# The last MLP group by seven half-size products too, and the second layer's norm on four engines

## The chip, the cores and the metric

The kernel runs on one core of one Trainium2 chip. The time is device microseconds of one execution, the median of the runs; the profile is of one further execution. The core has five engines with in-order queues of their own: TensorE (PE in the rows; PEld is its weight load), VectorE (DVE), ScalarE (ACT), GpSimd (POOL) and SyncE (SP), which issues the transfers.

## The reference, cut to what matters

The program is a two-layer trunk over 512 tokens of width 1024. Each layer has a mixer and an MLP, with a norm before each and a last norm behind the second layer. The change touches the MLPs, the norm before the second mixer (fox) and the last norm.

```python
def rmsnorm(x, g):
    xf = x.astype(jnp.float32)
    y = xf * lax.rsqrt(jnp.mean(xf * xf, axis=-1, keepdims=True) + RMS_EPS)
    return (y * g.astype(jnp.float32)).astype(x.dtype)

def sqrelu_mlp(h, w1, w2):
    a = jax.nn.relu(h @ w1)
    return (a * a) @ w2

def reference(x, ...):
    h = x
    for layer in range(DEPTH):
        hn = rmsnorm(h, mix_norm[layer])
        ...
        h = h + sqrelu_mlp(rmsnorm(h, mlp_norm[layer]), mlp_w1[layer], mlp_w2[layer])
    return rmsnorm(h, final_norm)
```

w1 is 1024 x 4096, w2 is 4096 x 1024, all in float32.

## The kernel before, in words

Every product is done as three matmuls in a reduced 32-bit format (mm3, L124 to L129): each operand is split into a high half (a copy that rounds, on ACT) and a low half (the operand less its high half, on DVE or POOL), and high x high, high x low and low x high are added up in PSUM. Weights come in by 512 KB loads on SP; split (L89, L92) makes both halves of a plain piece.

The residual stays in SBUF as four tiles x0 to x3 of 128 tokens x 1024. The stages follow each other: mixer of layer 0 (to about 295 us), its MLP (to about 635), the fox mixer of layer 1 (to about 875), its MLP (to about 1218), the tail. The order of instructions on each engine is set by the framework's scheduler from the program, its dependencies and a model of durations; prio() (L781) gives what is issued inside it precedence. An engine works through its queue in that order.

An MLP (mlp, L925) goes through 8 groups of 512 hidden columns. up(s) makes a group's activations in four blocks of 128 columns: 24 matmuls into a PSUM tile "acc", then relu on ACT (L971), a product with the row of inverse norms on POOL (L972), a square on ACT (L974). down(s) multiplies them by 512 rows of w2. For the groups 0 to 6 it does a 2 x 2 block product by seven half-size products in place of eight: combos makes sums and differences of the activations on POOL (L990 to L995) and splits each into halves on ACT (L980) and DVE (L398); weights makes those of w2 with additions on DVE (L1029) and splits on ACT (L1023) and DVE (L1024). A product is two tiles of tokens by 6 matmuls of 512 columns (L1069); where a PSUM bank holds a finished piece of the result, DVE adds it to the residual (L1077). Banks have the tags s, o, pt and acc. The products' order is 2, 1, 6, 7, 4, 5, 3, and product 2 is added up over the groups in two banks "pt". Group 7 is done by down_plain, a plain product, 4 tiles of tokens one behind the other, with additions at L1116. In the second layer finish makes the last norm of a tile behind its additions: inv_rms squares on ACT with a sum (L158), finds the inverse root by Newton steps of one column on DVE (L160 to L167), POOL multiplies by the final gain (L1086) and scales (L1089), and the last tile is scaled by ACT and DVE (L1093, L1094).

The norm before fox (norm_t, L370, and norm, L196) does one square of 1024 on ACT, the Newton steps, and two scalar_tensor_tensor on DVE (L200), which scale by the inverse norm and multiply by the gain at once. Then TensorE transposes (L386) and ACT and DVE make the halves xhi and xlo (L390, L391), from which fox's first projection starts.

## Time and profile before

| | us |
|---|---|
| median of 3 runs | 1227.72 (1227.18 to 1228.32) |
| the profiled execution | 1227.37 |
| its span | 1225.7 |
| TensorE busy in it | 1206.8 (98%) |
| DVE busy | 960.1 (78%) |
| ACT busy | 656.2 (54%) |
| POOL busy | 470.5 (38%) |

The span is the time from the first to the last instruction of the profiled execution; 1.67 us of its time lie outside. The mean granted clock of TensorE in it is 0.998 of full speed. Busy shares are means over stages with different limits.

### The profile page before, as it was taken

What the parts mean: (1) busy time and instruction counts of PE and PEld (TensorE: products, weight loads), DVE (VectorE), ACT (ScalarE), POOL (GpSimd) and SP (SyncE); (2) the same over time, 40 slices, a digit from 0 to 9 for tenths busy, and PEclk for the clock granted to TensorE, in tenths of its full rate; (3) what the DMA queues carried; (4) which work ended last, traced back from release to release, by engine and by line L of the source; (5) the groups of instructions that cost most, each with busy time, mean ns of one, the idle gap of its engine ahead of it and who ended that gap; (6) DMA issues with size and microseconds to landing.
All of it is one profiled execution on the core that took longest, in us unless ns stands there. A gap on an engine that the chain in (4) does not pass through costs nothing.

```text
span 1225.7 us, 17221 instructions
## 1 busy us (share of the span) xinstructions
PE 1206.8 (98%) x6215; PEld 1023.2 (83%) x6215; DVE 960.1 (78%) x1654; ACT 656.2 (54%) x1195; POOL 470.5 (38%) x483
## 2 busy tenths in 40 slices
PE   9999999999999999999999999999999999999997
PEld 7889987887888888888888898988788888888886
DVE  6877678788877987798875678548887798779875
ACT  6457666675554455445425666546455445544542
POOL 3534457542443224322103644435154323432314
PEclk9999999999999999999999999999999999999999
DMA  8962232130633333324015211321363333332201
GB/s 238 338 177 53 87 103 79 52 112 20 170 105 110 92 106 104 110 90 121 27 34 149 72 54 55 87 87 52 107 171 106 111 90 105 105 111 92 88 1 69
DMA packets 141968, 123.78 MB, mean 101 GB/s; under 512 B 6403, under 2 KB 117163, under 8 KB 141884
## 3 DMA queue, kind: packets, MB, share of 16 engines
q1 hardware_dynamic: 141724, 122.45, 34.0%
q8 instruction: 49, 0.80, 0.3%
q14 instruction: 35, 0.29, 0.1%
q10 hardware_dynamic: 160, 0.23, 0.1%
HBM read 120.27 MB, written 7.64 MB: 104 GB/s over the span
## 4 chain that ended last, share of the span: by engine, by line
PE 92%; DVE 5%; issue 1%; ACT 1%; DMA 1%; POOL 0%; DVEq 0%; ACTq 0%
PE acc L127 17%; PE acc L129 17%; PE acc L128 17%; PE s L1069 12%; PE o L1069 6%; PE s L415 4%; PE pt L437 3%; PE pt L1069 3%; PE o L450 2%; PE o L449 2%; DVE whl L92 1%; PE s L127 1%; PE s L128 1%; PE s L129 1%; PE pt L386 1%
## 5 line engine op out<-in xcount | busy, mean ns | idle before, releaser
L129 PE MATMUL acc<-xhi,whl 128*128 128x512 f32 (+1 forms) x768 | 294.9, 384 | 1.3 <-POOL whl L92 0.8
L127 PE MATMUL acc<-xhi,whl 128*128 128x512 f32 (+1 forms) x768 | 293.7, 383 | 0.7 <-DVE Q L400 0.5
L128 PE MATMUL acc<-xlo,whl 128*128 128x512 f32 (+1 forms) x768 | 293.3, 382 | 0.0
L92 DVE TENSOR_TENSOR whl<-raw,whl 128x1024 fp32r<-128x1024 f32 (+2 forms) x113 | 165.5, 1468 | 83.4 <-ACT whl L89 79.3
L972 POOL TENSOR_TENSOR r<-r,yrow 128x512 f32<-128x512 f32 x64 | 97.5, 1524 | 318.4 <-ACT r L971 315.9
L89 ACT ACTIVATE whl<-raw 128x1024 fp32r<-128x1024 f32 (+1 forms) x139 | 144.7, 1048 | 47.8 <-PE acc L129 31.1
L129 PEld LDWEIGHTS acc<-xhi,whl 128*128 128x128 f32 x768 | 144.6, 188 | 29.5 <-POOL whl L92 1.2
L127 PEld LDWEIGHTS acc<-xhi,whl 128*128 128x128 f32 x768 | 144.3, 188 | 28.3 <-PE acc L129 0.9
L1069 PE MATMUL s<-whl,sp 128*128 128x512 f32 x672 | 167.6, 390 | 0.0
L128 PEld LDWEIGHTS acc<-xlo,whl 128*128 128x128 f32 x768 | 144.8, 188 | 26.5
L1069 PEld LDWEIGHTS s<-whl,sp 128*128 128x128 f32 x672 | 126.2, 188 | 26.5
L1023 ACT ACTIVATE whl<-w 128x1024 fp32r<-128x1024 f32 x98 | 103.6, 1060 | 72.0 <-PE s L1069 44.3
L1024 DVE TENSOR_TENSOR whl<-w,whl 128x1024 fp32r<-128x1024 f32 x98 | 134.2, 1371 | 8.6 <-ACT whl L1023 8.6
L420 ACT ACTIVATE P<-P,sst 128x128 f32<-128x128 f32 (+3 forms) x160 | 88.9, 557 | 39.3 <-DVE sst L419 37.4
L971 ACT ACTIVATE r<-acc 128x512 f32<-128x512 f32 x62 | 37.1, 598 | 118.2 <-PE acc L129 118.2
L1069 PE MATMUL o<-whl,sp 128*128 128x512 f32 x336 | 88.8, 391 | 0.0
L439 ACT ACTIVATE PTh<-pt 128x512 fp32r<-128x512 f32 (+1 forms) x120 | 61.4, 523 | 49.4 <-PE pt L437 48.3
L440 DVE TENSOR_TENSOR PTl<-pt,PTh 128x512 fp32r<-128x512 f32 (+1 forms) x120 | 70.4, 596 | 20.7 <-ACT PTh L439 19.9
L92 POOL TENSOR_TENSOR whl<-raw,whl 128x1024 fp32r<-128x1024 f32 x26 | 64.3, 2476 | 54.6 <-ACT whl L89 54.0
L1029 DVE TENSOR_TENSOR w<-w,w 128x1024 f32<-128x1024 f32 x56 | 83.1, 1485 | 1.5 <-DMA w<-in_mlp_w 0.6
L422 POOL TENSOR_SCALAR P<-P,sst 128x128 f32<-128x128 f32 (+1 forms) x96 | 52.3, 550 | 70.7 <-DVE sst L421 64.8
L1077 DVE TENSOR_TENSOR x<-s,x 128x512 f32<-128x512 f32 x112 | 75.0, 682 | 3.0 <-PE s L1069 3.0
(279 smaller groups left out, 2429.3 us busy)
## 6 DMA issues: line engine op xcount, KB each, us to landing
raw<-in_mlp_w SPq DMA_DIRECT2D x72, 512.0 KB
w<-in_mlp_w SPq DMA_DIRECT2D x56, 512.0 KB
raw<-in_odd_w_in SPq DMA_DIRECT2D x22, 512.0 KB
raw<-in_even_w_in SPq DMA_DIRECT2D x20, 512.0 KB
band<-bias_dram SPq DMA_DIRECT2D x24, 256.0 KB
bias_dram<-bias_rows SPq DMA_DIRECT2D x16, 320.0 KB
raw<-in_even_w_out SPq DMA_DIRECT2D x8, 512.0 KB
raw<-in_odd_w_out SPq DMA_DIRECT2D x8, 512.0 KB
```

The costliest lines, as they stand in the source:

```text
L89: nc.scalar.activation(hl[:, 0, :n], raw[:, :n], AF.Copy)
L92: eng.tensor_tensor(hl[:, 1, :n], raw[:, :n], hl[:, 0, :n].bitcast(F32), op=ALU.subtract)
L127: mm(ps, ahl[0], bhl[0], start=first, stop=False)
L128: mm(ps, ahl[0], bhl[1], start=False, stop=False)
L129: mm(ps, ahl[1], bhl[0], start=False, stop=last)
L420: nc.scalar.activation(seg, seg, AF.Exp, bias=mn, scale=-1.0, accum_out=sm)
L972: nc.gpsimd.tensor_tensor(r, r, row, op=ALU.mult)
L1023: nc.scalar.activation(t[:, 0], src, AF.Copy)
L1024: nc.vector.tensor_tensor(t[:, 1], src, t[:, 0].bitcast(F32), op=ALU.subtract)
L1029: nc.vector.tensor_tensor(out, a_, b_, op=op)
L1069: mm = lambda l, r, first, last: nc.tensor.matmul(ps, l, r, start=first, stop=last, skip_group_check=True)
L1077: nc.vector.tensor_tensor(hv, ps, hv, op=ALU.add)
```

## The change

In both layers group 7 is now also done by the seven products, in the order 1, 2, 6, 7, 4, 5, 3 and with product 2 added to x0 and x1 there; down_plain is gone. In group 7 the low halves of the weights of products 6, 7, 4 and 5 are made by POOL in place of DVE. up is a generator, and the blocks 2 and 3 of group 7's up-projection are issued between products of group 6, behind products 1 and 7. The MLP's pool of weight halves has five buffers in place of three, that of activation halves ten in place of eleven. The last norm's pieces are two halves for every tile (before, the last tile had 512, 256 and 256); tiles 1 and 2 are scaled by ACT in place of POOL. The norm before fox squares in two halves into buffers of its own, multiplies by the gain on POOL and scales on ACT.

```diff
-    def inv_rms(self, h, cuts, sq_out):
+    def inv_rms(self, h, ranges, sq_out):
...
-    def norm(self, h, dst, g):
-
-        y = self.inv_rms(h, (0, D), lambda i: dst)
-        for c in (slice(0, D // 2), slice(D // 2, D)):
-            self.nc.vector.scalar_tensor_tensor(dst[:, c], h[:, c], y, g[:, c], op0=ALU.mult, op1=ALU.mult)
+    def norm(self, h, dst, g, sq_pool):
+
+        sq = [sq_pool.tile([P, S], F32, tag="sq", name=self.nm("sq")) for _ in range(2)]
+        y = self.inv_rms(h, [(0, S), (S, D)], lambda a, b: sq[a // S])
+        for c in (slice(0, S), slice(S, D)):
+            self.nc.gpsimd.tensor_tensor(dst[:, c], h[:, c], g[:, c], op=ALU.mult)
+            self.nc.scalar.activation(dst[:, c], dst[:, c], AF.Copy, scale=y)
...
-            mw = pool("mlpw", 3)
+            mw = pool("mlpw", 5)
             mr = pool("mlpraw", 5)
-            msp = pool("mlpsp", 11)
-            ml = pool("mlpl", 1)
+            msp = pool("mlpsp", 10)
...
-                return act
+                    yield act
...
-                def hl(src):
+                def hl(src, n):
                     t = mw.tile([P, 2, W_RAW], FR, tag="whl", name=self.nm("whl"))
                     with behind():
                         nc.scalar.activation(t[:, 0], src, AF.Copy)
-                        nc.vector.tensor_tensor(t[:, 1], src, t[:, 0].bitcast(F32), op=ALU.subtract)
+                        eng = nc.gpsimd if s == 7 and n in (6,7,4,5,) else nc.vector
+                        eng.tensor_tensor(t[:, 1], src, t[:, 0].bitcast(F32), op=ALU.subtract)
...
-                yield 2, hl(q[1, 2])
-                yield 1, hl(q[1, 1])
+                for i in ((1, 2) if s == 7 else (2, 1)):
+                    yield i, hl(q[1, i], i)
...
-            def down(s, act):
-                bs = combos(act)
+            def down(s, act, between=iter(())):
+                bs = combos(s, act)
                 bank = {}
+                end = s == 7
                 for n, w in weights(s):
                     where, opens, to = plan[n]
+                    if where == "y" and end:
+                        to = (0, 0)
...
+                            if to is not None:
+                                hv = hs[2 * to[1] + tt][:, S * to[0] + a:S * to[0] + b]
+                                with self.prio() if end and n in (4, 5, 3) else ExitStack():
+                                    nc.vector.tensor_tensor(hv, ps[:, a:b], hv, op=ALU.add)
+                        if tt and n in (1,7,):
+                            next(between, None)
+                        if end and final is not None and n in (4, 3):
+                            with self.prio() if n == 3 and tt else ExitStack():
+                                finish(2 * (n == 3) + tt, [(0, 512), (512, 1024)][::1 if n == 4 else -1])
...
-                        nc.gpsimd.tensor_scalar(xn[:, c], xn[:, c], y, 1.0, op0=ALU.mult, op1=ALU.mult)
+                        if t:
+                            nc.scalar.activation(xn[:, c], xn[:, c], AF.Copy, scale=y)
+                        else:
+                            nc.gpsimd.tensor_scalar(xn[:, c], xn[:, c], y, 1.0, op0=ALU.mult, op1=ALU.mult)
...
-            def down_plain(s, act):
...
-            prev = up(0)
+            *_, prev = up(0)
             for s in range(8):
-                nxt = up(s + 1) if s < 7 else None
-                (down if s < 7 else down_plain)(s, prev)
+
+                rest = up(s + 1) if s < 7 else iter(())
+                for _ in range(4 - 2 if s == 6 else 4):
+                    nxt = next(rest, None)
+                down(s, prev, rest)
```

In the changed kernel the matmul of the products stands at L1077, the addition to the residual at L1084, the weights' subtraction at L1028 and their additions at L1033, the activations' split at L981 and L400, the row product at L973, the combinations at L993 to L998, the last norm's product and scalings at L1098, L1102 and L1104.

The first place is DVE at the start of the second MLP (the first is alike), before. whl are weight halves, L92 those of the up-projection, L1024 those of the products of group 0, L1029 their sums.

```order
L1029 TENSOR_TENSOR w_1432_9319<-w_1434_9323,w_1432_9319 128x1024
L92 TENSOR_TENSOR whl_1401_9119<-raw_1400_9117,whl_1401_9119 128x1024
L1029 TENSOR_TENSOR w_1430_9315<-w_1430_9315,w_1432_9319 128x1024
L1024 TENSOR_TENSOR whl_1441_9363<-w_1432_9319,whl_1441_9363 128x1024
L92 TENSOR_TENSOR whl_1407_9155<-raw_1406_9153,whl_1407_9155 128x1024
L92 TENSOR_TENSOR whl_1411_9189<-raw_1410_9187,whl_1411_9189 128x1024
L92 TENSOR_TENSOR whl_1415_9223<-raw_1414_9221,whl_1415_9223 128x1024
```

The same place after the change (L1028 and L1033 are the lines that were L1024 and L1029).

```order
L1033 TENSOR_TENSOR w_1446_9359<-w_1445_9357,w_1446_9359 128x1024
L1033 TENSOR_TENSOR w_1445_9357<-w_1447_9361,w_1445_9357 128x1024
L92 TENSOR_TENSOR whl_1414_9157<-raw_1413_9155,whl_1414_9157 128x1024
L1033 TENSOR_TENSOR w_1443_9353<-w_1443_9353,w_1445_9357 128x1024
L1028 TENSOR_TENSOR whl_1454_9401<-w_1445_9357,whl_1454_9401 128x1024
L1028 TENSOR_TENSOR whl_1455_9418<-w_1446_9359,whl_1455_9418 128x1024
L1028 TENSOR_TENSOR whl_1458_9437<-w_1444_9355,whl_1458_9437 128x1024
L92 TENSOR_TENSOR whl_1420_9193<-raw_1419_9191,whl_1420_9193 128x1024
L92 TENSOR_TENSOR whl_1424_9227<-raw_1423_9225,whl_1424_9227 128x1024
L92 TENSOR_TENSOR whl_1428_9261<-raw_1427_9259,whl_1428_9261 128x1024
```

Three L1028 stand behind whl_1414, whose place was that of whl_1401, ahead of the next L92, where one L1024 stood.

The second place is DVE in the last group of the second layer, at the change from group 6 to group 7. Before, sp are activation halves, x0 to x3 the residual, s, o and pt PSUM banks:

```order
L1077 TENSOR_TENSOR x2_124<-s_1654_10839,x2_124 128x512
L398 TENSOR_TENSOR sp_1706_11247<-act_1663_10946,sp_1706_11247 128x512
L398 TENSOR_TENSOR sp_1707_11250<-act_1663_10946,sp_1707_11250 128x512
L1077 TENSOR_TENSOR x3_126<-s_1655_10847,x3_126 128x512
L1024 TENSOR_TENSOR whl_1699_11159<-w_1692_11115,whl_1699_11159 128x1024
L1077 TENSOR_TENSOR x0_107<-pt_1436_9327,x0_107 128x512
L1077 TENSOR_TENSOR x1_116<-pt_1437_9334,x1_116 128x512
L1024 TENSOR_TENSOR whl_1700_11176<-w_1693_11117,whl_1700_11176 128x1024
L1077 TENSOR_TENSOR x0_107<-s_1697_11140,x0_107 128x512
L398 TENSOR_TENSOR sp_1708_11253<-act_1664_10947,sp_1708_11253 128x512
L398 TENSOR_TENSOR sp_1709_11256<-act_1664_10947,sp_1709_11256 128x512
```

After:

```order
L1084 TENSOR_TENSOR x2_124<-s_1702_11108,x2_124 128x512
L400 TENSOR_TENSOR sp_1722_11288<-act_1677_10985,sp_1722_11288 128x512
L400 TENSOR_TENSOR sp_1723_11293<-t2_1720_11284,sp_1723_11293 128x512
L1084 TENSOR_TENSOR x3_126<-s_1703_11116,x3_126 128x512
L400 TENSOR_TENSOR sp_1724_11297<-act_1676_10984,sp_1724_11297 128x512
L1084 TENSOR_TENSOR x2_124<-s_1702_11108,x2_124 128x512
L400 TENSOR_TENSOR sp_1725_11301<-t2_1720_11284,sp_1725_11301 128x512
L400 TENSOR_TENSOR sp_1726_11304<-t1_1719_11283,sp_1726_11304 128x512
L1084 TENSOR_TENSOR x3_126<-s_1703_11116,x3_126 128x512
L400 TENSOR_TENSOR sp_1727_11307<-act_1677_10985,sp_1727_11307 128x512
L1084 TENSOR_TENSOR x0_107<-s_1734_11322,x0_107 128x512
L1084 TENSOR_TENSOR x0_107<-pt_1449_9365,x0_107 128x512
```

Behind these and two additions from bank o follows:

```order
L1084 TENSOR_TENSOR x3_126<-o_1740_11386,x3_126 128x512
L160 TENSOR_SCALAR nrm_1744_11406<-nrm_1744_11406 128x1
L1028 TENSOR_TENSOR whl_1749_11471<-w_1728_11310,whl_1749_11471 128x1024
L1084 TENSOR_TENSOR x1_116<-s_1735_11330,x1_116 128x512
L1084 TENSOR_TENSOR x0_107<-s_1734_11322,x0_107 128x512
```

Six subtractions of activation halves stand among the additions, where three stood between additions and two between weight subtractions; the additions x2 from s_1702 and x3 from s_1703 stand behind subtractions of combinations; the first Newton step stands ahead of the last L1028 and of the addition from s_1735.

The third place is POOL from the last row products on, before:

```order
L972 TENSOR_TENSOR r_1668_10978<-r_1668_10978,yrow_1389_8945 128x512
L972 TENSOR_TENSOR r_1672_11012<-r_1672_11012,yrow_1389_8945 128x512
L972 TENSOR_TENSOR r_1676_11046<-r_1676_11046,yrow_1389_8945 128x512
L972 TENSOR_TENSOR r_1680_11080<-r_1680_11080,yrow_1389_8945 128x512
L1086 TENSOR_TENSOR xn_1720_11307<-x0_107,gf_8953 128x512 x2
L1086 TENSOR_TENSOR xn_1725_11356<-x1_116,gf_8953 128x512 x2
```

After:

```order
L973 TENSOR_TENSOR r_1715_11227<-r_1715_11227,yrow_1402_8983 128x512
L994 TENSOR_TENSOR t2_1720_11284<-act_1677_10985,t1_1719_11283 128x512
L996 TENSOR_TENSOR act_1676_10984<-act_1677_10985,act_1676_10984 128x512
L1028 TENSOR_TENSOR whl_1737_11358<-w_1730_11314,whl_1737_11358 128x1024
L998 TENSOR_TENSOR t2_1720_11284<-act_1677_10985,t2_1720_11284 128x512
L1028 TENSOR_TENSOR whl_1738_11375<-w_1731_11316,whl_1738_11375 128x1024
L1028 TENSOR_TENSOR whl_1741_11394<-w_1729_11312,whl_1741_11394 128x1024
L1028 TENSOR_TENSOR whl_1748_11453<-w_1732_11318,whl_1748_11453 128x1024
L1098 TENSOR_TENSOR xn_1742_11404<-x0_107,gf_8991 128x512
L1098 TENSOR_TENSOR xn_1745_11432<-x1_116,gf_8991 128x512
```

Between the last row product and the products with the final gain now stand three combinations and four L1028 of 128 x 1024.

## Rows read from the trace of the kernel before

**Rows 1.** The page: its first line, TensorE in section 1, and the first line of section 4, the chain that ended last by engine.

```profile
span 1225.7 us, 17221 instructions
...
PE 1206.8 (98%) x6215; PEld 1023.2 (83%) x6215; DVE 960.1 (78%) x1654; ACT 656.2 (54%) x1195; POOL 470.5 (38%) x483
...
PE 92%; DVE 5%; issue 1%; ACT 1%; DMA 1%; POOL 0%; DVEq 0%; ACTq 0%
```

**Rows 2.** The table of waits of TensorE, its longest line: engine and line, what was waited for, us in total, times, longest.

```profile
PE acc L127 <- DVE x L476: 3.1, 5, 1.3
```

**Rows 3.** The chain that ended last, in order of time, at the end of the second MLP: start, us, what.

```profile
1177.04 2.72 PE pt L1069 x12
```

**Rows 4.** Windows of the core: from:to, length, then busy us and instructions of PE, PEld, DVE, ACT, POOL, the granted clock, the DMA share and GB/s. 598 to 617 and 1200 to 1218 are the last groups' plain products (1167 to 1200 has the end of group 6 in it), 617 to 640 the joint to fox.

```profile
598.00:617.00 19.00, 19.00 (x85) 15.74 (x84) 16.75 (x22) 8.29 (x9) 0.00 (x0) 1.00 0.00 1
617.00:640.00 23.00, 22.54 (x111) 18.75 (x111) 17.03 (x46) 6.31 (x12) 2.05 (x4) 1.00 0.04 9
...
1167.00:1200.00 33.00, 33.00 (x148) 27.30 (x146) 22.77 (x29) 12.73 (x16) 2.59 (x2) 1.00 0.00 0
```

**Rows 5.** Timelines of DVE and of POOL in a group of the second MLP: start, us, engine, line, operation, out<-in, shape, count, and in brackets the idle time before and what ended it.

```profile
976.12 1.54 DVE L1024 TENSOR_TENSOR whl<-w,whl 128x1024 fp32r<-128x1024 f32 x1 [0.69 <-ACT whl L1023]
977.59 0.68 DVE L1077 TENSOR_TENSOR x<-s,x 128x512 f32<-128x512 f32 x1
...
982.23 1.78 DVE L398 TENSOR_TENSOR sp<-act,sp 128x512 fp32r<-128x512 f32 x1
...
989.49 2.33 DVE L1024 TENSOR_TENSOR whl<-w,whl 128x1024 fp32r<-128x1024 f32 x1
...
976.54 2.28 POOL L993 TENSOR_TENSOR act<-act,act 128x512 f32<-128x512 f32 x1
981.25 2.21 POOL L995 TENSOR_TENSOR t<-act,t 128x512 f32<-128x512 f32 x1 [2.43 <-DVE sp L398]
989.30 1.43 POOL L972 TENSOR_TENSOR r<-r,yrow 128x512 f32<-128x512 f32 x1 [5.85 <-ACT r L971]
```

**Rows 6.** The instructions of one line over the whole run: engine, operation, count, then ns shortest/median/longest, first and last start, forms.

```profile
L1024 DVE TENSOR_TENSOR whl<-w,whl x98: 1209/1216/2331, 313.7 to 1189.1; 128x1024 fp32r<-128x1024 f32 x98
...
L398 DVE TENSOR_TENSOR sp<-act,sp x64: 677/936/1792, 331.2 to 1183.2; 128x512 fp32r<-128x512 f32 x64
...
L1077 DVE TENSOR_TENSOR x<-s,x x112: 674/681/692, 354.8 to 1197.9; 128x512 f32<-128x512 f32 x112
...
L92 POOL TENSOR_TENSOR whl<-raw,whl x26: 2372/2398/3182, 65.1 to 853.9; 128x1024 fp32r<-128x1024 f32 x26
```

**Rows 7.** The same view for the three instructions that make an activation block: relu, row product, square.

```profile
L971 ACT ACTIVATE r<-acc x62: 582/598/602, 317.5 to 1177.1; 128x512 f32<-128x512 f32 x62
...
L972 POOL TENSOR_TENSOR r<-r,yrow x64: 1288/1420/2307, 318.2 to 1177.8; 128x512 f32<-128x512 f32 x64
...
L974 ACT ACTIVATE act<-r x64: 621/634/636, 321.3 to 1179.1; 128x512 f32<-128x512 f32 x64
```

**Rows 8.** Timelines of DVE, ACT and TensorE at the joint from the first MLP to fox, as in rows 5. The last matmul of the MLP is that at 635.65.

```profile
632.68 1.41 DVE L200 SCALAR_TENSOR_TENSOR xn<-x,nrm,g 128x512 f32<-128x512 f32 x2
...
637.01 1.05 ACT L158 ACTIVATE xn<-x 128x1024 f32<-128x1024 f32 x1
637.96 0.19 ACT L158 ACTIVATION_READ_ACCUMULATOR xn<-x 128x1 f32 x1
638.05 1.14 ACT L390 ACTIVATE xhi<-pt 128x512 fp32r<-128x512 f32 x2
...
635.65 0.39 PE L129 MATMUL o<-whl,sp 128*128 128x512 f32 x1
635.88 1.04 PE L386 MATMUL pt<-ident,xn 128*128 128x128 f32 x8
637.17 0.39 PE L127 MATMUL acc<-whl,xhi 128*128 128x272 f32 x1 [0.25 <-ACT xhi L390]
...
638.64 0.29 PE L128 MATMUL acc<-whl,xhi 128*128 128x272 f32 x1
...
639.90 0.29 PE L127 MATMUL acc<-whl,xhi 128*128 128x272 f32 x1
```

**Rows 9.** The tail's timeline: the last matmul, the addition and square of the last 256 columns, the first and the last of the last tile's nine Newton steps, and the last issue of a transfer.

```profile
1217.71 0.28 PE L129 MATMUL s<-whl,sp 128*128 128x256 f32 x1
1218.03 0.42 DVE L1116 TENSOR_TENSOR x<-s,x 128x256 f32<-128x256 f32 x1 [0.16 <-PE s L129]
1218.54 0.42 ACT L158 ACTIVATE sq<-x 128x256 f32<-128x256 f32 x1 [0.92 <-DVE x L1116]
1219.09 0.21 DVE L162 TENSOR_SCALAR nrm<-nrm 128x1 f32<-128x1 f32 x1 [0.64 <-ACT sq L158]
...
1221.13 0.21 DVE L167 TENSOR_SCALAR nrm<-nrm 128x1 f32<-128x1 f32 x1
...
1222.14 0.38 ACTq L1095 DMA_DIRECT2D out<-xn  x1
```

**Rows 10.** Timelines of DVE and TensorE at the start of the second MLP. The matmul at 909.76 is the first of the next column block that needs the low half of its weights.

```profile
904.66 1.21 DVE L1024 TENSOR_TENSOR whl<-w,whl 128x1024 fp32r<-128x1024 f32 x1
905.80 4.54 DVE L92 TENSOR_TENSOR whl<-raw,whl 128x1024 fp32r<-128x1024 f32 x2
...
909.76 0.39 PE L129 MATMUL acc<-xhi,whl 128*128 128x512 f32 x1
```

More of the change, by code (lines that the diff above doesn't have):

```diff
@@ L155, in inv_rms @@
         m, y, u = (st[:, i:i + 1] for i in range(3))
-        sq = [st[:, 3 + i:4 + i] for i in range(len(cuts) - 1)]
-        for i, q in enumerate(sq):
-            nc.scalar.activation(sq_out(i), h[:, cuts[i]:cuts[i + 1]], AF.Square, accum_out=q)
+        sq = [st[:, 3 + i:4 + i] for i in range(len(ranges))]
+        for (a, b), q in zip(ranges, sq):
+            nc.scalar.activation(sq_out(a, b), h[:, a:b], AF.Square, accum_out=q)
         nc.vector.tensor_scalar(m, sq[0], 0.5 / D, 0.5 * RMS_EPS, op0=ALU.mult, op1=ALU.add)
@@ L368, in row_tile, with norm_t @@
         return g
[L370 removed]
+    def norm_t(self, hs, g, plain=False, sq_pool=None):
         nc = self.nc
@@ L380, in norm_t @@
             else:
-                self.norm(hs[t], xn, g)
+                self.norm(hs[t], xn, g, sq_pool)
             for j in range(2):
@@ L1064, in down @@
                             ps = bank[where, tt]
-                        for u in range(2):
-                            c = slice(256 * u + P * tt, 256 * u + P * tt + P)
-                            d = half[u]
-                            a_, b_ = (bs[n][:, 0, c], bs[n][:, 1, c]), (w[:, 0, d], w[:, 1, d])
-                            mm = lambda l, r, first, last: nc.tensor.matmul(ps, l, r, start=first, stop=last, skip_group_check=True)
-                            mm(a_[0], b_[0], opens and u == 0, False)
-                            mm(a_[0], b_[1], False, False)
-                            mm(a_[1], b_[0], False, u == 1)
@@ L1073, in down @@
-                        if where == "y" and s == 6:
-                            to = (0, 0)
-                        if to is not None:
-                            hv = hs[2 * to[1] + tt][:, half[to[0]]]
-                            nc.vector.tensor_tensor(hv, ps, hv, op=ALU.add)
-            def finish(t, cuts):
+                        for a, b in ((0, 512),):
+                            for u in range(2):
+                                c = slice(256 * u + P * tt, 256 * u + P * tt + P)
+                                d = slice(S * u + a, S * u + b)
+                                a_, b_ = (bs[n][:, 0, c], bs[n][:, 1, c]), (w[:, 0, d], w[:, 1, d])
+                                mm = lambda l, r, first, last: nc.tensor.matmul(ps[:, a:b], l, r, start=first, stop=last, skip_group_check=True)
+                                mm(a_[0], b_[0], opens and u == 0, False)
+                                mm(a_[0], b_[1], False, False)
+                                mm(a_[1], b_[0], False, u == 1)
+                            if to is not None:
+                                hv = hs[2 * to[1] + tt][:, S * to[0] + a:S * to[0] + b]
+                                with self.prio() if end and n in (4, 5, 3) else ExitStack():
+                                    nc.vector.tensor_tensor(hv, ps[:, a:b], hv, op=ALU.add)
@@ L1084, in finish @@
-                for i in range(len(cuts) - 1):
-                    sl = slice(cuts[i], cuts[i + 1])
+                y = self.inv_rms(hs[t], ranges, lambda a, b: sq[:, :b - a])
+                for a, b in ranges:
+                    sl = slice(a, b)
                     nc.gpsimd.tensor_tensor(xn[:, sl], hs[t][:, sl], gf[:, sl], op=ALU.mult)
```

42 lines of the change are left out of this document (12 added, 30 removed).

## The prediction

> **What bounds the kernel now.** I read the page first: TensorE is busy 1206.8 us of a span of 1225.7, and the chain of waits is 92% TensorE [rows 1]. The reader is to see that there is no second bound to trade against: what counts is how many matmuls there are, and each moment in which the engine has none ready. It stands for 1225.7 - 1206.8 = 18.9 us in all, of which 7.7 lie behind the last matmul; in the table of its waits, read next, the longest line is 3.1 us in five pieces, and belongs to the mixers [rows 2]. The chain over the end of the second MLP gives the price of a matmul: 12 of one product take 2.72 us, so 0.2267 us per 512 columns [rows 3]. The windows show how full the other engines are where the change works: in 598 to 617, the end of the first MLP, POOL does nothing and DVE 16.75 of 19 us; in 617 to 640 TensorE works 22.54 of 23 us, so the joint to the next stage costs 0.46 us today; the granted clock is 1.00 (the 2.4 GHz level) in all of them [rows 4].
>
> **How DVE and POOL share the stage.** This decides the case, so I looked at it in the timeline. At 976.12 DVE starts a weight subtraction and at 976.54 POOL a combination: POOL's takes 2.28 us, where this instruction alone takes 1.29. At 981.25 POOL starts first, and DVE's 512-wide subtraction at 982.23 takes 1.78 us in place of 0.68. At 989.30 POOL starts first and DVE's weight subtraction takes 2.33 in place of 1.21. The one that starts second ends about 0.13 us less than its own full length after the first has ended. An addition that reads PSUM, at 977.59, takes 0.68 beside a running POOL instruction [rows 5]. The counts agree over the whole run: the L1024 subtraction is 1209 to 2331 ns, L398 is 677 to 1792, but L1077, which reads PSUM, stays within 674 to 692 [rows 6]. So instructions of DVE and POOL with two operands in SBUF run one after the other.
>
> The Trainium skill says the same under "SBUF — State Buffer", section "Who interferes with whom": who issues first has the shared port pair for the whole instruction and the other is blocked. The trace has the second one start its work about 0.13 us before that; by the rule taken whole, each of some 12 meetings per layer would cost 0.13 us more, and the sum below some 3 us.
>
> **The change part by part.** The profiled execution took 1227.37 us (1.67 outside the span); the median of the runs shown is 1227.72. I sum against 1227.4.
>
> (1) Matmuls. The last group takes 7 x 12 = 84 in place of 96 in each layer: 24 x 0.2267 = -5.4 us, all on the path, as TensorE is full there.
>
> (2) The last group's feed, per layer. Today the last group needs no combinations, and POOL is empty behind its four row products [rows 4]. In the changed order POOL runs, behind the last row product, three combinations and four weight subtractions. A combination is 1.29 us by the shortest row of the same form, a weight subtraction on POOL 2.39 (L92's shortest and median, 2372 and 2398 ns) [rows 6]: 3 x 1.29 + 4 x 2.39 = 13.4 us. They start when the last activation is there: from T0, the end of the up-projection's last matmul, relu 0.60, row product 1.29, square 0.63 [rows 7], so T0 + 2.5. Between them DVE has seven 512-wide subtractions of 0.69, of which five meet POOL and take 0.42 each from it (0.69 less the overlaps and the copies that ACT does first): POOL is done at T0 + 2.5 + 13.4 + 2.1 = T0 + 18. TensorE has from T0 on 24 matmuls of group 6's products 4 and 5, 24 of its product 3 and of group 7's product 2, then 2 + 6 + 10 of products 7 and 1: 66 x 0.2267 = 15.0 us, and then needs the bank that DVE empties behind its subtraction for product 5 (sp_1726 in the order of DVE). That subtraction waits for POOL's third one, and the bank is free at T0 + 16.0 to 16.7: a stall of 1.0 to 1.7, I take 1.7, as DVE is second to start at every one of these meetings. The next bank stands behind the last 512-wide subtraction, T0 + 19.6 by the same count; by then TensorE has spent 15.0 + 1.7 + 6 x 0.2267 = 18.1: another 1.5. With 0.1 for the last subtraction itself 3.3 per layer, 6.6 for both. Below: 0, if DVE gets in between two POOL instructions each time. Above: every one of five DVE subtractions behind a full 2.39, on TensorE's path 5.5 per layer.
>
> The Trainium skill, "Perfetto Trace Analysis", section "Optimizing Scalar/DVE Operations", warns against this very step: GpSimd and DVE share a read port, so moving work from one to the other might not help. By it moving the four subtractions is worth nothing; by the rows it is a loss, since the same work takes 2.39 on POOL against 1.21 on DVE, and the other engine waits through it.
>
> (3) Newton steps between the evacuations. DVE's new order puts the start of the first tile's norm (L160) ahead of the last weight subtraction and of an addition that frees a bank of product 6. It waits for ACT's square, 0.63 + 0.19 [rows 7, 8], behind an addition of 0.68: 1.5 us in which DVE stands and TensorE soon does too; in both layers: +3.0. Below 0, if TensorE is still late from (2); above 2 x 2.3, all nine steps, 1219.09 to 1221.34 [rows 9].
>
> (4) The norm into the second layer. For one tile it is not shorter: today a square of 1.05, Newton, and two DVE products of 1.41 [rows 8]; then two squares of 0.63 + 0.19, Newton, and two scalings of about 0.60 on ACT. The products with g go to POOL beside it. But it loads ACT, which works in order: tile 1's scalings stand behind the square of tile 3's half, which ends last. From E, the end of the last product: addition 0.68, square 0.82, two scalings 1.2, so E + 2.7; transposes; meanwhile on ACT another square 0.82 and tile 2's scalings 1.2, then two copies 1.14 and a DVE subtraction that reads PSUM, about 0.69: E + 6.5. TensorE has its eight transposes (1.04) and, from 637.17 or E + 1.1 on, 24 matmuls of 272 columns of 0.126 (ten from 638.64 to 639.90) [rows 8], and is through at E + 4.2: 2.3 late; for tile 2 behind it I add 0.6, an estimate of half of one copy and subtraction; less the 0.46 of today: +2.4. Below -0.5; above 4.6, twice the one stall.
>
> (5) The start of each MLP. With five weight buffers in place of three DVE does two more subtractions (L1028) ahead of the weights of the up-projection's fifth column. Today that weight's low half is there at about 908.1 (one half of the 4.54 from 905.80) and is wanted at 909.76 [rows 10]: 1.6 us to spare. Two more take 2 x 1.21 = 2.4 or, beside POOL, 2 x 2.33 = 4.7: late by 0.8 to 3.1. I take 0.8, as the row nearest to the place, 904.66, took 1.21; twice: +1.6. Below 0: TensorE has no use for the halves that come early.
>
> (6) The tail. Today 4.15 us pass from the end of the last matmul (1217.71 + 0.28) to the last issue at 1222.14 [rows 9]. The last piece is 512 wide in place of 256: addition 0.68 for 0.42 [rows 6, 9], square 0.63 for 0.42, +0.5. Tiles 2 and 3 now end 6 matmuls apart, and their Newton steps alternate on DVE: some five foreign steps of about 0.25 (nine take 2.25) in tile 3's chain, +1.2. Sum +1.7; below 0.5, above 2.4 with one of tile 2's scalings ahead on ACT.
>
> The loads bring the same bytes (four pieces of 512 KB in place of four rows' of 512 KB), and in the windows of both last groups the DMA share is 0.00 [rows 4], so nothing is late there; the squares' two buffers of their own take nothing from anyone. Both at 0.
>
> Sum: -5.4 + 6.6 + 3.0 + 2.4 + 1.6 + 1.7 = +9.9, so 1227.4 + 9.9 = 1237.3 us.
>
> **The rivals.**
> A, the cover holds (faster). TensorE is full today with DVE at 16.75 of 19, and POOL idle: work for POOL could be free. If DVE's subtractions go in pairs between POOL's, the banks come some 1.7 earlier and (2) and (3) vanish, while (4), (5), (6) cost 0.5, 0, 1.2: -5.4 + 1.7 = 1223.7. The point from which it decides: the product-5 bank free before T0 + 15. Against it: in the rows the one in front held every time. Chance 0.15.
> B, half of each stall is hidden behind the others, as a late TensorE needs less: half of the 15.3 of (2) to (6), -5.4 + 7.6 = +2.2, at about 1229; with a little less it is no change. Chance 0.18.
> C, the meetings cost more: (2) at 5.5 per layer, (5) at 3.1, (4) at 4.6: -5.4 + 11 + 3 + 4.6 + 6.2 + 1.7 = +21, 1248. For it: L972 rows reach 2307 [rows 7]. Chance 0.17.
> My forecast has 0.50.
>
> **How the numbers follow.** What a measurement can tell here is about 0.2%, 2.5 us, so 1225.3 to 1230.2 is no change. A is faster; B falls half within that and otherwise just above or below it: faster 0.15 + 0.03, same 0.10, slower 0.72. The range runs from 1223.5 (A's own time) to 1247 (C's).
>
> **What would show it.** In the profile of the changed kernel: waits of TensorE for DVE's additions (L1084) in the last group of both layers, about 3 us each; DVE's L400 rows of 1.5 to 3 us and POOL's L1028 of 2.4 to 3.1 there; a wait for xhi or xlo (L392, L393) of some 3 us at the joint; a wait for L92 at the MLPs' starts; 4.15 grown to about 5.9 at the tail. If TensorE has no waits in the last groups and L400 is near 0.69 there, step (2) is wrong, and A holds. If the joint shows no new wait, (4) is.

## The result, and the profile after

The changed kernel takes 1240.73 us (median of 4 runs, 1240.41 to 1241.27), the kernel before 1227.45 in the same comparison: 1.0104 times as long, 95% interval 1.0088 to 1.012. It is slower by some 13.3 us, where I had forecast 1237.3. The profiled execution took 1241.27 us.

The page of the changed kernel, its first line, TensorE in section 1 and the chain that ended last:

```profile
span 1239.2 us, 17234 instructions
...
PE 1205.8 (97%) x6179; PEld 1016.0 (82%) x6179; DVE 951.5 (77%) x1668; ACT 672.2 (54%) x1225; POOL 504.3 (41%) x502
...
PE 89%; DVE 8%; ACT 2%; issue 1%; DMA 0%; POOL 0%; DVEq 0%; ACTq 0%
```

Against [rows 1] TensorE has less to do and stands more: of the chain 89% are left where it had 92, and DVE has 8% in place of 5. The mean granted clock is 0.998 as before, so nothing of this is the clock. Where TensorE waits now, in the table of its waits (what was waited for, us in total, times, longest):

```profile
PE s L1077 <- DVE x L1084: 7.5, 6, 1.4
PE acc L129 <- DVE whl L92: 3.6, 3, 1.6
PE acc L127 <- DVE x L478: 3.1, 5, 1.3
...
PE acc L127 <- ACT xhi L392: 1.5, 2, 0.9
```

The line that led the table before [rows 2] is now the third (L478, 3.1 us again). New are the additions that free the banks of the products (three waits in each layer), the weights at the start of each MLP (two waits of 1.6), and the joint to fox. The table counts from the modelled end of a matmul, which lies some 0.16 us behind the moment at which the next could have begun, so each wait costs a little more than it shows.

The last group of the second layer, first TensorE: start, us, count, and the wait ahead in brackets. (A row of several begins at the first one's start.)

```profile
1210.65 1.76 PE L1077 MATMUL o<-whl,sp 128*128 128x512 f32 x7
1213.81 1.66 PE L1077 MATMUL s<-whl,sp 128*128 128x512 f32 x6 [1.40 <-DVE x L1084]
1216.60 1.66 PE L1077 MATMUL s<-whl,sp 128*128 128x512 f32 x6 [1.13 <-DVE x L1084]
1218.09 2.93 PE L1077 MATMUL o<-whl,sp 128*128 128x512 f32 x12
1220.89 3.06 PE L1077 MATMUL s<-whl,sp 128*128 128x512 f32 x12
...
1225.31 4.58 PE L1077 MATMUL s<-whl,sp 128*128 128x512 f32 x18 [1.36 <-DVE x L1084]
```

Then DVE and POOL over the same stretch:

```profile
1202.72 2.88 DVE L400 TENSOR_TENSOR sp<-t,sp 128x512 fp32r<-128x512 f32 x1
...
1208.05 5.11 DVE L400 TENSOR_TENSOR sp<-t,sp 128x512 fp32r<-128x512 f32 x2
1213.07 0.68 DVE L1084 TENSOR_TENSOR x<-s,x 128x512 f32<-128x512 f32 x1
1213.67 2.27 DVE L400 TENSOR_TENSOR sp<-act,sp 128x512 fp32r<-128x512 f32 x1
1215.87 0.68 DVE L1084 TENSOR_TENSOR x<-s,x 128x512 f32<-128x512 f32 x1
...
1199.69 1.30 POOL L994 TENSOR_TENSOR t<-act,t 128x512 f32<-128x512 f32 x1 [0.74 <-ACT act L975]
...
1202.20 2.86 POOL L1028 TENSOR_TENSOR whl<-w,whl 128x1024 fp32r<-128x1024 f32 x1
...
1206.93 8.46 POOL L1028 TENSOR_TENSOR whl<-w,whl 128x1024 fp32r<-128x1024 f32 x3
```

This is [rows 5] on a larger scale. Four of DVE's six subtractions in this stretch, 0.68 us by themselves, take 2.3 to 2.9 us, each beside one of POOL's four weight subtractions, and these take 2.85 in place of 2.39, since each waits for a DVE subtraction in its turn. The additions L1084 take their usual 0.68, but stand in DVE's order behind the L400: those at 1213.07 and 1215.87 end just before TensorE goes on at 1213.81 and 1216.60 (the third wait, at 1225.31, has another cause; see point 3 below). The chain over 1200 to 1217 says it in its first line:

```profile
by line: DVE sp L400 73.3%; DVE x L1084 22.4%; PE s L1077 6.7%; issue 0.3%
```

The start of the second MLP, DVE and then TensorE, to compare with [rows 10]:

```profile
910.73 5.70 DVE L1028 TENSOR_TENSOR whl<-w,whl 128x1024 fp32r<-128x1024 f32 x3
916.35 4.53 DVE L92 TENSOR_TENSOR whl<-raw,whl 128x1024 fp32r<-128x1024 f32 x2
...
916.73 0.39 PE L128 MATMUL acc<-xlo,whl 128*128 128x512 f32 x1
```

Three subtractions for the products take 5.70 us where one of 1.21 stood, and the weights of the fifth column block come behind them; the matmul after the one at 916.73 waits 1.6 us. The joint, TensorE, to compare with [rows 8]:

```profile
642.72 0.39 PE L127 MATMUL acc<-whl,xhi 128*128 128x272 f32 x1 [0.60 <-ACT xhi L392]
...
648.21 0.39 PE L127 MATMUL acc<-whl,xhi 128*128 128x272 f32 x1 [0.85 <-ACT xhi L392]
```

And the tail, to compare with [rows 9]:

```profile
1229.05 0.84 PE L1077 MATMUL s<-whl,sp 128*128 128x512 f32 x3
1229.93 0.69 DVE L1084 TENSOR_TENSOR x<-s,x 128x512 f32<-128x512 f32 x1
...
1233.43 1.33 ACT L1102 ACTIVATE xn<-xn,nrm 128x512 f32<-128x512 f32 x2 [0.77 <-DVE nrm L167]
...
1234.67 0.65 ACT L1108 ACTIVATE xn<-xn,nrm 128x448 f32<-128x448 f32 x1
1235.35 0.39 ACTq L1110 DMA_DIRECT2D out<-xn  x1
```

From the last matmul's end, 1229.05 + 0.84 = 1229.89, to the last issue are 5.46 us, against 4.15.

### The profile page after: what moved, and what is told of

Its sections match the earlier page's. It is cut to its first block, busy times and chain, and to the rows that moved or that the text cites. A ratio compares the mean times of both kernels' runs of the same rounds, so it can differ in the third digit from the quotient of the medians.

```text
span 1239.2 us, 17234 instructions
## 1 busy us (share of the span) xinstructions
PE 1205.8 (97%) x6179; PEld 1016.0 (82%) x6179; DVE 951.5 (77%) x1668; ACT 672.2 (54%) x1225; POOL 504.3 (41%) x502
## 4 chain that ended last, share of the span: by engine, by line
PE 89%; DVE 8%; ACT 2%; issue 1%; DMA 0%; POOL 0%; DVEq 0%; ACTq 0%
PE acc L127 17%; PE acc L129 17%; PE acc L128 17%; PE s L1077 12%; PE o L1077 6%; PE s L417 4%; PE pt L439 3%; PE pt L1077 3%; DVE sp L400 2%; PE o L452 2%; PE o L451 2%; DVE x L1084 1%; DVE whl L92 1%; PE pt L388 1%; PE o L290 1%
## 5 line engine op out<-in xcount | busy, mean ns | idle before, releaser
L92 DVE TENSOR_TENSOR whl<-raw,whl 128x1024 fp32r<-128x1024 f32 (+1 forms) x105 | 150.9, 1443 | 105.8 <-ACT whl L89 87.1
L973 POOL TENSOR_TENSOR r<-r,yrow 128x512 f32<-128x512 f32 x64 | 91.0, 1423 | 344.0 <-ACT r L972 279.6
L1077 PE MATMUL s<-whl,sp 128*128 128x512 f32 x768 | 192.2, 392 | 7.5 <-DVE x L1084 7.5
L1077 PEld LDWEIGHTS s<-whl,sp 128*128 128x128 f32 x768 | 143.4, 188 | 41.7 <-DVE x L1084 11.4
L89 ACT ACTIVATE whl<-raw 128x1024 fp32r<-128x1024 f32 (+1 forms) x131 | 136.5, 1048 | 35.0 <-PE acc L129 31.3
L1028 DVE TENSOR_TENSOR whl<-w,whl 128x1024 fp32r<-128x1024 f32 x104 | 134.0, 1302 | 13.8 <-ACT whl L1026 13.5
L1026 ACT ACTIVATE whl<-w 128x1024 fp32r<-128x1024 f32 x112 | 116.4, 1057 | 49.0 <-PE s L1077 23.3
L1084 DVE TENSOR_TENSOR x<-s,x 128x512 f32<-128x512 f32 x128 | 85.9, 680 | 13.2 <-PE s L1077 13.2
L1077 PE MATMUL o<-whl,sp 128*128 128x512 f32 x384 | 93.8, 391 | 0.0
L92 POOL TENSOR_TENSOR whl<-raw,whl 128x1024 fp32r<-128x1024 f32 x26 | 64.4, 2480 | 52.6 <-ACT whl L89 39.4
L1077 PEld LDWEIGHTS o<-whl,sp 128*128 128x128 f32 x384 | 71.8, 188 | 16.1 <-POOL whl L1028 0.9
```

Source lines behind the costliest of these rows:

```text
L89: nc.scalar.activation(hl[:, 0, :n], raw[:, :n], AF.Copy)
L92: eng.tensor_tensor(hl[:, 1, :n], raw[:, :n], hl[:, 0, :n].bitcast(F32), op=ALU.subtract)
L973: nc.gpsimd.tensor_tensor(r, r, row, op=ALU.mult)
L1026: nc.scalar.activation(t[:, 0], src, AF.Copy)
L1028: eng.tensor_tensor(t[:, 1], src, t[:, 0].bitcast(F32), op=ALU.subtract)
L1077: mm = lambda l, r, first, last: nc.tensor.matmul(ps[:, a:b], l, r, start=first, stop=last, skip_group_check=True)
```

## The experiments

All are the changed kernel with the edit shown. Times are medians; ratios are to the kernel before in the same comparison (its median is 1227.24 in the first four, 1227.77 in e5 to e8, 1227.51 in the last two) and are not exactly the quotients of the medians. An edit can also change the order that the scheduler gives to DVE and TensorE; where that matters it is said. Where the text says what a run won or lost in one stretch, it compares when TensorE starts the same matmul in the two profiled executions.

**All low halves on DVE (e1).**

```diff
-                        eng = nc.gpsimd if s == 7 and n in (6,7,4,5,) else nc.vector
+                        eng = nc.gpsimd if s == 7 and n in () else nc.vector
```

> The changed kernel with one thing undone: in group 7 all low halves of the weights are made by DVE, none by POOL. Theory of the meetings (POOL's four 2.39 us subtractions hold DVE's subtractions up, and the additions that free TensorE's banks stand behind those): the waits of TensorE for L1084 in both last groups (2.9 and 1.2 to 1.5 us each) go, DVE's L400 falls back to about 0.7; TensorE then comes to the joint some 5 us earlier than the norm does and waits there more, and the tail is longer: about 1234, 6 us less than the changed kernel. Rival (DVE is the engine that is short in the last group, and POOL relieves it): 4 x 1.21 us per layer come back to DVE, so 1240.7 + up to 9.7, 1245 to 1250. Second rival (the last group is late for want of activations, whoever makes the low halves): 1240 to 1241, with the waits where they are.

1235.37 us, ratio 1.0069 (1.0054 to 1.0085). No wait for L1084 is left in the upper lines of the table; in their place stand, at the joint,

```profile
PE pt L388 <- ACT xn L202: 2.4, 1, 2.4
PE acc L127 <- ACT xhi L392: 1.7, 1, 1.7
```

So POOL did not relieve DVE: giving DVE 4.8 us of work back in each layer makes the kernel 5.4 us faster. In the profiled execution the products of the two MLPs take 4.8 and 5.3 us less than in the changed kernel, but 3.2 us of that are lost at the joint, where TensorE now waits for the tiles' norms, and 1.0 in the tail. At the joint the clock falls as well, once TensorE has stood 2.4 us, worked 1.3 us and stood again: to 0.50 (the 1.2 GHz level), as this window shows (from:to, length, then busy us and count of PE, PEld, DVE, ACT and POOL, granted clock, DMA share, GB/s):

```profile
640.80:643.30 2.50, 2.50 (x11) 2.27 (x12) 1.53 (x4) 2.50 (x5) 0.00 (x0) 0.50 0.82 214
```

This run changes the order too: at the end of each MLP six matmuls of TensorE stand elsewhere, and on DVE more does. So it does not show by itself that the meetings are the cause; e9 does.

**Nearly the same POOL time, one operand (e2).**

```diff
-                        eng.tensor_tensor(t[:, 1], src, t[:, 0].bitcast(F32), op=ALU.subtract)
+                        if s == 7 and n in (6,7,4,5,):
+                            for _ in range(2):
+                                nc.gpsimd.tensor_scalar(t[:, 1], t[:, 0].bitcast(F32), 0.0, 1.0, op0=ALU.mult, op1=ALU.mult)
+                        else:
+                            nc.vector.tensor_tensor(t[:, 1], src, t[:, 0].bitcast(F32), op=ALU.subtract)
```

> The changed kernel, but POOL's four low-half subtractions per layer in group 7 are each replaced by two multiplications by zero with one input (tensor_scalar, 128 x 1024), so POOL is busy about as long in the same places and products wait for it as before, but it takes no second operand. This leaves the low halves of these four weight pieces out of the result. Theory of the meetings: an instruction of POOL with one input does not hold DVE up, so L400 is about 0.7 there and the group's waits go: 1230 to 1234. Rival (POOL is merely slow, and the products wait for the halves that it makes): 1240 to 1242, the same waits.

1231.40 us, ratio 1.0033 (1.002 to 1.0046), and no wait for the additions is left in the table; 0.9 us in two waits for the halves that POOL makes are new. POOL's slowness as such costs little. (TensorE and ACT keep the order of the changed kernel here; on DVE one instruction per layer stands elsewhere.) But the mechanism I gave was wrong in one point, as the timelines of POOL and DVE show:

```profile
1197.41 1.50 POOL L1029 TENSOR_SCALAR whl<-whl 128x1024 fp32r<-128x1024 f32 x1
1200.79 8.89 POOL L1029 TENSOR_SCALAR whl<-whl 128x1024 fp32r<-128x1024 f32 x7
...
1197.92 1.53 DVE L400 TENSOR_TENSOR sp<-t,sp 128x512 fp32r<-128x512 f32 x1
...
1201.89 2.38 DVE L400 TENSOR_TENSOR sp<-t,sp 128x512 fp32r<-128x512 f32 x2
```

The subtraction at 1197.92 takes 1.53 us beside a POOL instruction with one operand: that too holds it up. The difference is the length of one hold, 8.89 / 7 = 1.27 us here, 2.85 there; DVE gets in behind it. The runs in pieces, below, take this up.

**The old norm (e3).**

```diff
-        y = self.inv_rms(h, [(0, S), (S, D)], lambda a, b: sq[a // S])
+        y = self.inv_rms(h, [(0, D)], lambda a, b: dst)
...
-            self.nc.gpsimd.tensor_tensor(dst[:, c], h[:, c], g[:, c], op=ALU.mult)
-            self.nc.scalar.activation(dst[:, c], dst[:, c], AF.Copy, scale=y)
+            self.nc.vector.scalar_tensor_tensor(dst[:, c], h[:, c], y, g[:, c], op0=ALU.mult, op1=ALU.mult)
```

> The changed kernel with the norm before fox as it was (one square of 1024 on ACT, two scalar_tensor_tensor on DVE). My prediction's step 4 (the new norm costs 2.4 us at the joint, because of ACT's order): 1238.3. Rival (the joint is late because all four tiles end late in the seven-product form, whichever norm follows): 1240 to 1242, no change, with other waits of the same sum at the joint.

1241.53 us, ratio 1.012 (1.0105 to 1.0135): no gain. Which norm follows does not matter to the changed kernel, and my step 4 falls.

**Three weight buffers in group 0 (e4).**

```diff
-            mw = pool("mlpw", 5)
+            mw = pool("mlpw", 3)
+            mx = pool("mlpx", 2)
...
-                    t = mw.tile([P, 2, W_RAW], FR, tag="whl", name=self.nm("whl"))
+                    t = (mx if s >= 1 and n in (6, 4) else mw).tile([P, 2, W_RAW], FR, tag="whl", name=self.nm("whl"))
```

> The changed kernel, but two of the five weight buffers are used from group 1 on only (for products 6 and 4); group 0 has three, as before the change. Theory (the two more early subtractions of group 0 stand ahead of the up-projection's weights on DVE, 1.76 us of wait per layer): the waits for L92 at both MLPs' starts go, 3.5 us less, and with other buffers the order in the last group may shift by 1 to 2 us: 1235.5 to 1238. Rival (the weights of the up-projection come late from DMA or ACT): 1240 to 1241, waits unchanged.

1235.38 us, ratio 1.0069 (1.0052 to 1.0086). DVE's order at the start of the second MLP has one subtraction for the products again, and the waits for L92 there are gone:

```profile
909.64 1.21 DVE L1029 TENSOR_TENSOR whl<-w,whl 128x1024 fp32r<-128x1024 f32 x1
910.77 4.54 DVE L92 TENSOR_TENSOR whl<-raw,whl 128x1024 fp32r<-128x1024 f32 x2
```

That is 5.3 us in all, more than the 3.2 of the two waits, because the last groups changed too: their waits for the additions sum to 5.4 us (3.3 in banks s, 2.1 in banks o) in place of 7.5. In the profiled execution the starts are 1.9 us shorter each and the products of the two MLPs 2.1 together; 1.5 of that go at the joint, where TensorE waits longer and its clock falls as in e1.

**Both undone (e5), the first layer only (e6), plain in both layers (e7).** e5 has the edits of e1 and e4. e6 does group 7 of the second layer by the plain product again, e7 that of both layers (the interleaving and the place of product 2 go back with it, and in e7 the two later buffers hold products 7 and 4):

```diff
-                down(s, prev, rest)
+                if s == 7 and layer in (1,):
+                    down_plain(s, prev)
+                else:
+                    down(s, prev, rest)
```

> The changed kernel with the two undone together: low halves of group 7 on DVE, and three weight buffers in group 0 (two more, for products 6 and 4, from group 1 on). Theory (meetings and starts are separate losses at separate places): 5.4 + 5.3 off 1240.7, so 1229 to 1231; TensorE stands less than 1 us at each place in the last groups, and what is left over the kernel before stands at the joint (1.5 to 3 us) and in the tail (about 2 us). Rival (the two remove the same waits, those of a full DVE): 1233 to 1235.

> As the run with both repairs, but the second layer's group 7 is done by the plain product as before the change, so only the first layer has 12 matmuls fewer. Theory (in the second layer the 2.7 us of matmuls are given back in waits in front of group 7 and in the longer tail): as fast as with seven products in both layers or up to 1.5 us faster, 1228 to 1230. Rival (the matmuls saved in the second layer come through once the meetings are gone): 2 to 2.7 us slower than the run with both repairs, 1232 to 1233.

> As the run with both repairs, but group 7 plain in both layers: of the change only the norm on four engines, the interleaved buffers and the order of helpers stay. Theory (the new norm behind a plain last group costs nothing, tiles ending one by one): 1227 to 1229. Rival (the new norm itself costs what my step 4 said, 2.4 us): 1229.5 to 1231.

e5 took 1230.13 us, ratio 1.002 (1.001 to 1.003); e6 1228.50, 0.9996 (0.9985 to 1.0007); e7 1227.78, 0.9997 (0.9989 to 1.0006). The two gains add up in the total: 13 us go down to under 3. Stretch by stretch they do not: the products of the MLPs win 6.7 us together against the changed kernel, where e1 alone won 10.1, while the joint and the tail lose nothing here. e7 shows that the new norm and the new buffers cost nothing behind a plain last group. But none is faster than the kernel before, though e5 has 24 matmuls fewer. Its last matmuls, and its first wait at the joint:

```profile
1213.81 4.24 PE L1078 MATMUL s<-whl,sp 128*128 128x512 f32 x18
...
636.06 1.27 PE L388 MATMUL pt<-ident,xn 128*128 128x128 f32 x8 [0.86 <-ACT xn L202]
```

TensorE ends at 1213.81 + 4.24 = 1218.05, where it ended at 1217.99 before [rows 9]: of the 5.4 us of saved matmuls some 4 have gone in the last groups, into waits of 0.1 to 0.5 us with a slower start behind each, and the joint with the next stage is 1.6 longer. The tail behind is longer by what it was in the changed kernel; in e6 and e7, where the second layer's group 7 is plain, it is as short as before (7.96 and 7.94 us from the last matmul's start to the end, 7.94 before).

**Three weight buffers throughout (e8).**

```diff
-            mw = pool("mlpw", 5)
+            mw = pool("mlpw", 3)
```

> The changed kernel with three weight buffers throughout in place of five. Theory (the starts' waits come from the two more buffers, but the last group needs them to have its halves made ahead of the products): the waits for L92 at the starts go, 3.5 us, and the last groups lose several us more each, since POOL's subtractions cannot begin before products of group 7 free buffers: 1245 to 1255. Rival (the two more buffers only do harm): 1236.5 to 1238.

1259.38 us, ratio 1.0233 (1.0204 to 1.0262), more than I expected. The waits at the starts are gone, but others are longer:

```profile
PE s L1077 <- DVE x L1084: 14.6, 5, 4.6
PE pt L388 <- ACT xn L202: 6.0, 1, 6.0
```

In the last group of the second layer POOL's four weight subtractions start 10.0 to 26.4 us behind its first combination (1225.29 to 1241.69, behind 1215.33), where they came 2.5 to 12.9 us behind it in the changed kernel: ACT's copies for three of them wait until a product of TensorE is done and its buffer free. The longest wait there is a meeting again, now also with a sum of weights on DVE (DVE, then POOL):

```profile
1224.76 3.49 DVE L400 TENSOR_TENSOR sp<-t,sp 128x512 fp32r<-128x512 f32 x2
1228.18 3.36 DVE L1033 TENSOR_TENSOR w<-w,w 128x1024 f32<-128x1024 f32 x1
...
1225.29 5.16 POOL L1028 TENSOR_TENSOR whl<-w,whl 128x1024 fp32r<-128x1024 f32 x2 [2.74 <-ACT whl L1026]
```

Against the changed kernel the products lose 12.1 us together and the starts win 3.8, which is within what I expected. Beyond it are the joint, 8.0 us, where a long wait is paid twice (last section), and 4.6 us in the first mixer, which the edit does not touch: there DVE's L92 starts at 65.24, 0.01 us behind one of POOL's, and takes 3.44 us, where in the changed kernel it was the first of the two and took 1.22. That part is chance, and the profiled execution is the slowest of the four (1253.05 to 1262.37). The two more buffers are needed by the last group and in the way in the first.

**POOL's work in pieces (e9 in two, e10 in four, with 256 for 512).**

```diff
-                        eng.tensor_tensor(t[:, 1], src, t[:, 0].bitcast(F32), op=ALU.subtract)
+                        cut = 512 if eng is nc.gpsimd else W_RAW
+                        for a in range(0, W_RAW, cut):
+                            eng.tensor_tensor(t[:, 1, a:a + cut], src[:, a:a + cut], t[:, 0, a:a + cut].bitcast(F32), op=ALU.subtract)
```

> The changed kernel, but each of POOL's four low-half subtractions per layer in group 7 is issued as two of 128 x 512 in place of one of 128 x 1024; the same work on the same engine. Theory (what counts is how long one instruction of POOL holds DVE's two-operand subtractions up: the run without second operands showed L400 at up to 1.8 us beside one-operand POOL instructions of 1.27, and no waits of TensorE): the holds go from 2.85 to about 1.3 to 1.6 us, the waits for L1084 in the last groups shrink to well under half, 1234 to 1237. Rival (DVE and POOL share one path, so the sum of their work decides and not its pieces): 1240 to 1242. Second rival (the run without second operands was quick since a one-operand instruction hardly holds DVE up at all, and a two-operand one does whatever its length): 1239 or more, with L400 of 2.5 us and over.

> As the run in halves, with four pieces of 128 x 256 each. Theory of the holds: pieces of 0.73 us, so L400 at up to about 1.4 us; a further 0 to 3 us less than halves, 1231 to 1236 (more fixed time on POOL against shorter holds). Rival (sum of work): 1241 to 1244, as POOL's sum grows by 16 fixed times.

e9 took 1234.81 us, ratio 1.0062 (1.0045 to 1.0078), e10 1235.21, 1.0069 (1.0051 to 1.0088). The same subtractions on the same engine, only in halves, save 6 us; quarters save no more in the total. The longest L400 of all is now 1.79 us, where it was 2.9:

```profile
L400 DVE TENSOR_TENSOR sp<-t,sp x48: 675/680/1792, 336.0 to 1205.5; 128x512 fp32r<-128x512 f32 x48
```

and the waits for the addition fall from 7.5 us in six to 3.2 in four (e9) and 1.4 in one (e10). e9 is the cleanest of the runs: DVE, ACT and TensorE go through the same lines, tiles and shapes in the same order as in the changed kernel, from the first instruction to the last, and only POOL's pieces differ. In its second layer the first of the three waits is gone, the second is down from 1.13 to 0.34, and the third stays:

```profile
1214.37 3.02 PE L1079 MATMUL s<-whl,sp 128*128 128x512 f32 x12 [0.34 <-DVE x L1086]
...
1218.51 3.68 PE L1079 MATMUL s<-whl,sp 128*128 128x512 f32 x14 [1.12 <-DVE x L1086]
```

It is the length of a single hold that put the additions of the first two waits too late, not the sum of the two engines' work. In e9 the products of the two MLPs win 2.4 and 3.2 us and nothing else is touched but 1.2 us in the first mixer, by chance. In e10 they win 3.6 and 5.7, so the shorter pieces do help there; but TensorE comes earlier to the joint and loses 1.5 us, with the clock at the lower level as in e1, and the tail is 2.7 us longer, where POOL's last product with the gain (L1100, at 1225.04) comes late. e10's order on DVE and TensorE differs too, so what the quarters win by themselves is not shown.

## Why the prediction was right, point by point

The time was right within 3.4 us, and its largest term for the reason given, the meetings of DVE and POOL in the last groups. Of the other steps (3) came at another place than I had named, (4) was wrong in its cause and near in its size by luck, and (5) was mis-sized.

(1) Matmuls, -5.4: as counted; the price per matmul is unchanged (12 in 2.93 - 0.16 us or a little over).

(2) The feed of the last group, +3.3 per layer. With the last activation there at 1199.69, T0 is 1199.69 - 2.5 = 1197.2. POOL was to be done at T0 + 18 and was at 1206.93 + 8.46 = T0 + 18.2; the first bank was to be free at T0 + 16.0 to 16.7 and was at 1213.75, T0 + 16.6; the next at T0 + 19.6, and was at 1216.55, T0 + 19.4. The two stalls, start to start: 1213.81 less (1210.65 + 7 x 0.2267) is 1.6, predicted 1.7; 1216.60 less (1213.81 + 6 x 0.2267) is 1.4, predicted 1.5. e1 and e2 fit the cause and e9 shows it. Rival A fell at the point it named.

(3) Newton steps, +3.0 for both: the third wait, 1.36 us at 1225.31, and 1.04 in the first layer; start to start 1.5 and 1.2. The kind was right and the size near, but the place was another. The L160 that I named, at 1218.38, waits for nothing. What delays TensorE are the steps behind it, two of which wait for ACT's squares, between two additions:

```profile
1221.95 0.68 DVE L1084 TENSOR_TENSOR x<-o,x 128x512 f32<-128x512 f32 x1
1222.82 0.15 DVE L160 TENSOR_SCALAR nrm<-nrm 128x1 f32<-128x1 f32 x1 [0.19 <-ACT sq L158]
1223.76 0.21 DVE L162 TENSOR_SCALAR nrm<-nrm 128x1 f32<-128x1 f32 x1 [0.78 <-ACT sq L158]
...
1224.57 0.68 DVE L1084 TENSOR_TENSOR x<-s,x 128x512 f32<-128x512 f32 x1
```

This wait is not lateness left over from (2): in e9, with the same order and (2) nearly gone, it stays at 1.12 and 1.38 us. It goes in e1 and e2.

(2) and (3) together were 9.6 for both layers, 4.8 for one; from 1210.65 to 1229.89 the 61 matmuls of the rows would take 61 x 0.2267 + 0.16 = 14.0 us and took 19.2, so 5.2 in the second layer, and by the same count 4.8 in the first (621.74 to 641.24). The extra is some 0.1 us behind each wait and between products.

(4) The norm into the second layer, +2.4: this step failed in its cause, the order of ACT in the new norm. The joint lost 0.60 + 0.85 + 0.2 + 0.2 us in place of 0.46, so +1.4 in waits and, with what is slower behind each, +2.0 on TensorE; but e3 has the old norm and is no faster, and e7 has the new norm and is as fast as before. What costs is the seven-product form, whichever norm follows. The likely reason, which no run changes by itself, is that the tiles end late: the last additions to x0 to x3 are done at 634.1, 637.3, 640.6 and 642.0, before at 623.6, 625.9, 631.3 and 636.8. When TensorE comes earlier, as in e1, it waits 2.4 + 1.7 us there.

(5) The starts, +1.6: mis-sized. They cost 1.6 each in the table, 3.2 in all, and 1.9 each on TensorE. I counted two more subtractions at 1.21; the three there took 5.70 together, so 4.5 for the other two if one took its 1.21, since POOL was at work beside them. That is the case I had priced at 2 x 2.33 and did not take. My upper bound was 3.1 per start.

(6) The tail, +1.7: 5.46 - 4.15 = 1.3 to the last issue, and 0.3 more behind it. That it is the wider last piece and the alternating steps was not tested apart; that it comes with the seven products in the second layer, e6 and e7 show.

All of the 13.6 us by which the profiled execution's span grew can be placed, by when TensorE starts the first matmul of each stretch (us):

| stretch on TensorE | before | after | longer by | forecast |
|---|---|---|---|---|
| mixer of layer 0 | 294.83 | 295.66 | 0.8 | 0 |
| starts of the two MLPs, up to the first product | 54.44 and 54.42 | 56.34 and 56.30 | 3.8 | 1.6 |
| products of the two MLPs | 286.61 and 286.64 | 289.09 and 289.35 | 5.2 | 4.2 |
| joint and fox | 240.77 | 242.76 | 2.0 | 2.4 |
| last matmul's start to the end | 7.94 | 9.72 | 1.8 | 1.7 |

The forecast of the products is (1) to (3) together, -5.4 + 9.6. The 0.8 of the mixer, most of it one wait (L817, 1.3 us for 0.6 at L815), is chance: in the runs e1 to e7, e9 and e10 this stretch takes between 294.4 and 296.1. So the starts are the term that missed most.

Rival B was half right in its idea: e1 and e10 show that what TensorE wins in the last groups is partly given back further on, but in the changed kernel the stalls were hardly hidden behind each other. Two slips have no bearing on the argument: the bounds of the range were put at 1223.5 and 1247, where the sums of A and C give 1223.7 and 1248; and the list of DVE's order before the change has four subtractions of activation halves, two and two, not the five of the sentence under it.

## What to carry to other kernels

Before work is moved from DVE to POOL, count what DVE does with two operands in SBUF in that stretch and what POOL reads from SBUF there, with one operand or two, and look at what stands behind the shorter ones in DVE's queue; if POOL must have some, give it short pieces. A spare buffer is used by the scheduler wherever it can be, also where the early work stands ahead of something urgent. A product with fewer matmuls that ends all its outputs together may give back, at the next stage and in the tail, what a plainer one earned by ending them one by one. And time that is won ahead of a joint counts only as far as the next stage is ready for it: e1 and e10 won more in the last groups than e9 and were no faster.

## What the runs showed of the hardware

A POOL instruction with one SBUF operand holds up a DVE subtraction with two as well: 1.53 us in place of 0.68 at 1197.92 in e2. The Trainium skill says so on its page "SBUF — State Buffer", section "Who interferes with whom": a DVE instruction with two SBUF inputs contends with a GpSimd instruction that reads SBUF. The trace agrees, here for one that reads a single operand, and my expectation for e2 had left it out.

A hold lasts for one instruction: in e9 the six pieces of POOL from 1203.72 follow each other without a gap, and DVE's subtractions among them take 1.1 to 1.8 us, where they took 2.3 to 2.9 beside pieces of twice the width.

In e8 a long wait was paid twice. TensorE stood 4.39 us and then worked at the lower clock for a while; its timeline, and two windows (length, then busy us and count of PE, PEld, DVE, ACT, POOL, granted clock, DMA share, GB/s):

```profile
633.52 4.60 PE L1077 MATMUL s<-whl,sp 128*128 128x512 f32 x12 [4.39 <-DVE x L1084]
```

```profile
633.80:637.30 3.50, 3.50 (x10) 2.69 (x10) 1.91 (x4) 0.99 (x1) 1.27 (x1) 0.52 0.00 0
637.50:641.00 3.50, 3.50 (x17) 2.89 (x16) 2.17 (x4) 0.50 (x1) 3.50 (x2) 1.00 0.00 0
```

12 matmuls took 4.60 us in place of 2.88, at a granted clock of 0.52 (the 1.2 GHz level), and then 1.00 came back. Behind the waits of 1.4 us in the changed kernel the clock stays at 1.00 (mean of 1205 to 1230). It fell at the joint too, in e1 (where TensorE stood 2.4 and 1.7 us), e4 (0.8 and 1.0) and e10 (0.8 and 1.1): there the mean granted clock from 640 to 650 us is 0.83. In the changed kernel (0.6 and 0.9) and in e5 (0.9 and 0.4) it is 1.00.
